# Gathering experts' tokens for two pairs at once from an fp32r copy of h, and scattering a pair's output in one block

## The chip, the cores and the metric

One core of a Trainium2 chip runs the whole kernel. The metric is the time of one execution in microseconds (us), the median of several runs. Lower is better.

## The reference

Two layers work on 512 tokens of 1024 channels in fp32. Each layer has a mixer (attention beside a convolution in the first, a short convolution in the second) and then a mixture of 16 experts in which each expert chooses its own 64 tokens. The change concerns the experts alone:

```python
def ec_moe(h, w_r, w_gate, w_up, w_down):
    bsz, n, _ = h.shape
    cap = max(1, EC_CAPACITY * n // N_EXPERTS)          # 2 * 512 // 16 = 64
    aff = jax.nn.softmax(jnp.einsum("bnd,de->bne", h, w_r).astype(jnp.float32), axis=-1)
    gates, idx = lax.top_k(jnp.swapaxes(aff, 1, 2), cap)
    bidx = jnp.broadcast_to(jnp.arange(bsz)[:, None, None], idx.shape)
    xs = h[bidx, idx]
    hid = jax.nn.silu(jnp.einsum("becd,edf->becf", xs, w_gate)) * jnp.einsum("becd,edf->becf", xs, w_up)
    ys = jnp.einsum("becf,efd->becd", hid, w_down) * gates[..., None].astype(h.dtype)
    return jnp.zeros_like(h).at[bidx, idx].add(ys)
# per layer: h = h + m5 * ec_moe(modulate(rms_norm(h), m3, m4), ...)
```

## The kernel before

Tokens lie on the partitions in four tiles of 128 (`h[t]`). In each layer `moe` first routes: VectorE finds every expert's 64 tokens and gives each chosen token a place from 1 to 64 (`slot`). Experts then go in eight pairs, expert 0 to 15 in order. `one_hot(pair)` makes a matrix of zeros and ones that picks a pair's 2 x 64 tokens; `gather` multiplies h (for the first pair h with the norm's factor in the matrix, afterwards `xr2`, a copy of h times that factor) by it on TensorE and gets the pair's tokens, channels on the partitions, in `xs`; a VectorE pass per 128 channels adds scale and shift (line 1094). An expert's gate and up products (`halves`, line 1124) read `xs` against the weights, `hid` is made, transposed (line 1166) and multiplied by the down weights. `spread` transposes the one-hot matrix into `C` and sums the pair's gates; `scatter` adds the finished pair's output back to `h`, two TensorE passes at a time between the down products of the next even expert (line 1175).

Weights come in loads of 1 MB (256 rows of a 1024 x 1024 matrix). An expert has twelve: gate 0 to 3, up 4 to 7, down 8 to 11; "load n" below counts them through a layer from 0, so expert e has loads 12e to 12e+11. All are issued by SyncE (SP) in that order, far ahead of their use: an issue waits only until the buffer that it writes is no longer read. Buffers come from three pools: `ring` (5), `w` (3) and `big` (9), and for loads 2 and 3 from `p`. `SLOT` deals them out:

```python
j = (i if i < 2 else i - 2 if i < 17 else i - 4) % 15
return BIG(shape) if i in (17, 18) or j >= 8 else RING(shape) if j < 5 else W(shape)
```

So loads 0 to 18 have buffers of their own (all 9 of `big` among them), and from load 19 on a cycle of 15 runs: 5 `ring`, 3 `w`, 7 `big`. The two others of `big` hold `xr2` from expert 1 on. From load 27 on, load n waits until TensorE has read load n - 15 (loads 19 to 26 wait for one read earlier still). The order of work on each engine is the order in which the code is written (`manual_schedule`).

Of the kernel before, what the change touches and what calls it, by code (L numbers as in the profile page):

```python
# [50 lines left out]
def backbone(ctx, tc, x, c, cx, c_ctx, ada_w, ada_b, norm1_g, norm2_g, ev_w_in, ev_q_g, ev_k_g,  # L51
# [66 lines left out]
    def EARLY(*dims):  # L118
        """What only the first mixer needs; its buffer goes to the experts' weights afterwards."""
# [367 lines left out]
    # every step of the mixer by name, with the steps that must be emitted before it  # L487
# [70 lines left out]
    # rms over heads, rope  # L558
# [412 lines left out]
    def moe(l, setup, route):  # L971
# [14 lines left out]
        afp = SM([128, NT, 32], tag="af", bufs=1)  # token tiles in the order 0, 2, 1, 3  # L986
# [11 lines left out]
        # an expert's 64th largest: each half of the tokens (its own partitions) in falling order, then  # L998
        # max(A[i], B[63 - i]) are the 64 largest of both
# [24 lines left out]
        # how many are larger, in every partition: their count on the diagonal, summed over the partitions  # L1024
# [4 lines left out]
        # the larger ones count first, then those equal to it; a count above 64 gets no place  # L1029
# [19 lines left out]
        xr2 = []  # L1049

        def one_hot(pair, scale=None):
            m_ = T([128, NT, 128])
            for t in range(NT):
                for par in range(2):
                    e = 2 * pair + par
                    o = m_[:, t, par * 64:par * 64 + 64]
                    if scale is None:
                        dve.tensor_scalar(o, iota[:, 1:65], slot[:, t, e:e + 1], None, op0=OP.is_equal)
                    else:
                        dve.tensor_scalar(o, iota[:, 1:65], slot[:, t, e:e + 1], scale(t, e), op0=OP.is_equal,  # L1060
                                          op1=OP.mult)
            return m_

        def spread(pair, m_):
            p = PB([128, NT, 128])
            for t in range(NT):
                pe.transpose(p[:, t], m_[:, t], ident)
# [315 lines left out]
```

## Time and profile before

| what | value |
|---|---|
| median of 3 runs (lowest, highest) | 1653.07 us (1652.53, 1658.62) |
| span of the profiled execution, first to last instruction | 1649.7 us |
| median time less that span | 3.4 us |
| TensorE busy | 1495.5 us, 91% of the span |
| VectorE, ScalarE, GpSimd busy | 43%, 17%, 16% |
| moved by DMA | 488.79 MB, mean 296 GB/s |

The profiled execution's own time is not listed apart; its span is 3.4 us under the median of the runs, which is taken here as what lies around the span. Busy time of TensorE is modelled from the starts of its instructions, so it says that work was queued, not that it ran at peak. The experts of the first layer take the stretch from about 424 to 910 us, those of the second that from 1148 to 1635 us.

### The profile page before, as it was taken

Reading aid. Unit: us, or ns where it says so; the run is one execution under the profiler, and the core shown is the slowest. Engines: PE = TensorE matmul, PEld = TensorE weight load, DVE = VectorE, ACT = ScalarE, POOL = GpSimd, SP = SyncE. Lnnn points to the kernel's source line nnn. Section 1 sums busy time; section 2 is a strip of 40 time slices with the busy share of each in tenths; the row PEclk is TensorE's granted clock in tenths of the full one; section 3 lists DMA queues with packets and bytes.
Section 4 is the critical chain, followed back from the end, with each engine's and each line's share of the span. In section 5 each row is a group of like instructions: output and inputs, shape, how many; then the busy total and the mean of one; then the engine's idle time right before and its main releaser. Section 6 shows DMA issues by size and latency. Waiting matters only on the chain. (4 is left out here: it accounts for less than half of the span.)

```text
span 1649.7 us, 19217 instructions
## 1 busy us (share of the span) xinstructions
PE 1495.5 (91%) x7771; PEld 811.8 (49%) x7771; DVE 716.2 (43%) x1421; ACT 287.8 (17%) x489; POOL 263.3 (16%) x199
## 2 busy tenths in 40 slices
PE   4887989888799999999998799996999999999995
PEld 2676644477443444344342577795444344434431
DVE  1999757543422323322321899525123232332223
ACT  2423223333010000010000422221110000001002
POOL 1656233531000000000000434440000000000001
PEclk9998979889799999999999999997999999999998
DMA  9643214045799999999999247538799999999993
GB/s 326 242 158 115 90 51 153 0 179 194 293 339 411 408 409 409 409 409 409 409 409 392 94 172 264 176 131 328 264 397 409 409 409 409 409 409 409 409 407 131
DMA packets 143795, 488.79 MB, mean 296 GB/s; under 512 B 7756, under 2 KB 35708, under 8 KB 137564
## 3 DMA queue, kind: packets, MB, share of 16 engines
q1 hardware_dynamic: 142976, 486.57, 76.3%
q8 instruction: 61, 1.00, 0.2%
q0 software_dynamic: 336, 0.85, 0.2%
q10 hardware_dynamic: 396, 0.16, 0.0%
q14 instruction: 26, 0.21, 0.0%
HBM read 485.45 MB, written 2.10 MB: 296 GB/s over the span
## 5 line engine op out<-in xcount | busy, mean ns | idle before, releaser
L1124 PE MATMUL pb<-big,t 128*64 128x512 f32 x912 | 200.8, 592 | 0.0
L1150 DVE TENSOR_TENSOR t<-t,pb 128x512 f32<-128x512 f32 x32 | 22.0, 688 | 332.9 <-PE pb L1124 311.0
L1124 PE MATMUL pb<-ring,t 128*64 128x512 f32 x704 | 157.8, 595 | 2.3 <-DMA ring<-in_moe_w_up_dram 2.3
L1105 DVE TENSOR_TENSOR hall<-hall,pb 128x512 f32<-128x512 f32 x128 | 87.3, 687 | 111.7 <-PE pb L1104 111.7
L350 POOL TENSOR_TENSOR w<-ring,w 128x1024 fp32r<-128x1024 f32 x44 | 111.8, 2550 | 122.1 <-ACT w L349 122.1
L1124 PEld LDWEIGHTS pb<-big,t 128*64 128x64 f32 x912 | 65.5, 137 | 130.2 <-issue 124.5
L1124 PE MATMUL pb<-big,p 128*64 128x512 f32 x464 | 113.9, 606 | 5.7 <-ACT p L1168 5.7
L350 POOL TENSOR_TENSOR w<-big,w 128x1024 fp32r<-128x1024 f32 x10 | 24.6, 2481 | 569.3 <-DMA ring<-in_ada_w_dram 525.2
L373 PE MATMUL pa<-w,big 128*128 128x256 f32 x368 | 106.8, 290 | 1.3 <-DVE big L739 0.8
L1091 PEld LDWEIGHTS pa<-t,big 128*128 128x128 f32 x896 | 101.1, 192 | 11.4 <-issue 11.4
L477 DVE SCALAR_TENSOR_TENSOR t<-t,ring,t 128x497 f32<-128x497 f32 (+14 forms) x116 | 106.5, 982 | 0.1
L375 PE MATMUL pa<-w,big 128*128 128x256 f32 x368 | 105.2, 286 | 0.6 <-DVE big L363 0.4
L374 PE MATMUL pa<-w,big 128*128 128x256 f32 x368 | 105.2, 286 | 0.0
L1091 PE MATMUL pa<-t,big 128*128 128x128 f32 x896 | 103.8, 277 | 0.0
L373 PE MATMUL pb<-big,w 128*128 128x512 f32 x248 | 99.8, 402 | 3.5 <-DVE big L362 3.2
L375 PE MATMUL pb<-big,w 128*128 128x512 f32 x248 | 98.7, 398 | 2.5 <-POOL w L350 2.5
L1124 PEld LDWEIGHTS pb<-ring,t 128*64 128x64 f32 x704 | 50.0, 138 | 102.8 <-issue 91.5
L374 PE MATMUL pb<-big,w 128*128 128x512 f32 x248 | 98.7, 398 | 1.4 <-POOL big L363 1.2
L1104 PE MATMUL pb<-p,t 128*128 128x512 f32 x256 | 92.8, 448 | 5.1 <-ACT p L1080 3.9
L1181 DVE TENSOR_TENSOR p<-pb,G 64x512 f32<-64x512 f32 x60 | 41.3, 688 | 117.1 <-PE pb L1124 100.4
L1124 PE MATMUL pb<-w,t 128*64 128x512 f32 x400 | 89.5, 593 | 0.0
L1094 DVE TENSOR_SCALAR t<-pa,a,mT 128x128 f32<-128x128 f32 x128 | 44.3, 404 | 94.7 <-PE pa L1091 94.7
(289 smaller groups left out, 2055.5 us busy)
## 6 DMA issues: line engine op xcount, KB each, us to landing
big<-in_moe_w_gate_dram SPq DMA_DIRECT2D x60, 1024.0 KB, 18.3
big<-in_moe_w_down_dram SPq DMA_DIRECT2D x58, 1024.0 KB, 18.3
big<-in_moe_w_up_dram SPq DMA_DIRECT2D x54, 1024.0 KB, 18.3
ring<-in_ada_w_dram SPq DMA_DIRECT2D x48, 1024.0 KB, 6.8
ring<-in_moe_w_up_dram SPq DMA_DIRECT2D x48, 1024.0 KB, 18.2
ring<-in_moe_w_down_dram SPq DMA_DIRECT2D x42, 1024.0 KB, 18.3
ring<-in_moe_w_gate_dram SPq DMA_DIRECT2D x40, 1024.0 KB, 18.3
w<-in_moe_w_down_dram SPq DMA_DIRECT2D x28, 1024.0 KB, 18.3
```

Of the source, the lines that this page charges most:

```text
L350: pool.tensor_tensor(lo, src, hi.bitcast(F32), op=OP.subtract)
L373: pe.matmul(o, ah, bh, start=first and i == 0, stop=False)
L374: pe.matmul(o, ah, bl, start=False, stop=False)
L375: pe.matmul(o, al, bh, start=False, stop=last and i == n - 1)
L477: dve.scalar_tensor_tensor(acc, gp[:, a + k - MID:b + k - MID], vcT[:, k * 4 + j:k * 4 + j + 1], acc, op0=OP.mult, op1=OP.add)
L1091: pe.matmul(pa[k // 4][:, k % 4], (xr2 if pair else h)[t][:, k * 128:(k + 1) * 128], Pm[:, t], start=(t == 0), stop=(t == NT - 1))
L1094: dve.tensor_scalar(xs[k // 4][:, k % 4], pa[k // 4][:, k % 4], a2[:, k:k + 1], sh2[:, k:k + 1], op0=OP.mult, op1=OP.add)
L1104: pe.matmul(p, C[:, t * 128:(t + 1) * 128], y[:, dh], start=(y is yh), stop=(y is yl))
L1105: dve.tensor_tensor(h[t][:, ds], h[t][:, ds], p, op=OP.add)
L1124: pe.matmul(ps[64 * f:64 * f + 64, :], lhs, w[:, f * 512:(f + 1) * 512], start=(k == 0), stop=(k == KD - 1), tile_position=(0, 64 * f))
L1150: dve.tensor_tensor(hid, sl.rearrange("p (a b) -> p a b", b=128), pgu[1].rearrange("p (a b) -> p a b", b=128), op=OP.mult)
L1181: dve.tensor_tensor(y[ps_, dh], po[hs], G5[hs, ds], op=OP.mult)
```

## The change

The gather works for groups of pairs: pair 0 alone, then pairs 1 and 2, 3 and 4, 5 and 6, then pair 7 alone. `terms` keeps h times the norm's factor as two fp32r terms (`xh2`, and what is left in `xl2`) in four buffers of `big` where `xr2` had two, and a gather multiplies both terms by a one-hot matrix of up to 256 columns. `SLOT` deals loads from 19 on in a cycle of 13 (5 `ring`, 3 `w`, 5 `big`). The first pair's one-hot matrix is made without the norm's factor and then multiplied by it (`gather_first`). One VectorE operation compares all of a matrix's columns of a token tile. The gates are also split in two fp32r terms (`afs`). A pair's scatter stands in one block between the next even expert's up products and its transposes (`scatter_rows`, two banks of PSUM and one add per token tile). A group's last pair has its `spread` in its odd expert. The loads' issues are written ahead of their use by `load_next`; their order on SP is as before.

```diff
@@ SLOT
         j = (i if i < 2 else i - 2 if i < 17 else i - 4) % 15
+        if i > 18:
+            j = (i - 19) % 13
         return BIG(shape) if i in (17, 18) or j >= 8 else RING(shape) if j < 5 else W(shape)
@@ moe
-        xr2 = []
+        xh2, xl2 = [], []
+        afs = SM([128, NT, 2, NE], F32R, tag="afs", bufs=1)
+        dve.tensor_copy(afs[:, :, 0], af)
+        dve.tensor_tensor(afs[:, :, 1], af, afs[:, :, 0].bitcast(F32), op=OP.subtract)
+        def one_hot(p0, n):
+            ms = [T([128, 2, n * 128], F32R) for _ in range(2)]
+            for t in range(NT):
+                o = ms[t // 2][:, t % 2].rearrange("p (e s) -> p e s", s=64)
+                dve.tensor_tensor(o, iota[:, None, 1:65].to_broadcast([128, 2 * n, 64]),
+                                  slot[:, t, 2 * p0:2 * p0 + 2 * n][:, :, None].to_broadcast([128, 2 * n, 64]),
+                                  op=OP.is_equal)
+            return ms
@@ spread
-                pe.matmul(pg, m_[:, t], af[:, 2 * (t % 2) + t // 2, 2 * pair:2 * pair + 2], start=(t == 0), stop=(t == NT - 1))
+                pe.matmul(pg, ms[t // 2][:, t % 2, c], afs[:, 2 * (t % 2) + t // 2, :, 2 * pair:2 * pair + 2],
+                          start=(t == 0), stop=(t == NT - 1))
@@ gather
+        def gather_first(ms):
+            m_ = T([128, NT, 128])
+            for t in range(NT):
+                dve.tensor_scalar(m_[:, t], ms[t // 2][:, t % 2].bitcast(F32), rstd[:, t:t + 1], None, op0=OP.mult)
...
+        def terms():
+            for x in (xh2, xl2):
+                xr = [BIG([128, 2, D], F32R) for _ in range(2)]
+                x += [xr[t // 2][:, t % 2] for t in range(NT)]
+            for t in range(NT):
+                act.activation(xh2[t], h[t], AF.Copy, scale=rstd[:, t:t + 1])
+                dve.scalar_tensor_tensor(xl2[t], h[t], rstd[:, t:t + 1], xh2[t].bitcast(F32), op0=OP.mult,
+                                         op1=OP.subtract)
+        def gather(ms, n):
+            pa = [PA([128, 4, n * 128]) for _ in range(2)]
+            xs = [C4([128, 2, 256]) for _ in range(4)]
+            for k in (0, 2, 4, 6, 1, 3, 5, 7):
+                for t in range(NT):
+                    for x in (xh2, xl2):
+                        pe.matmul(pa[k // 4][:, k % 4], x[t][:, k * 128:(k + 1) * 128], ms[t // 2][:, t % 2],
+                                  start=(t == 0 and x is xh2), stop=(t == NT - 1 and x is xl2))
+                modulated(pa, xs, k, n * 128)
+            return xs
@@ scatter
+        def scatter_rows(C, yh, yl, t):
+            p = PA([128, 2, 512])
+            for dh in range(2):
+                for y in (yh, yl):
+                    pe.matmul(p[:, dh], C[:, t * 128:(t + 1) * 128], y[:, dh], start=(y is yh), stop=(y is yl))
+            dve.tensor_tensor(h[t], h[t], p.rearrange("p a b -> p (a b)"), op=OP.add)
@@ loop over pairs and experts
+        groups = {0: 1, 1: 2, 3: 2, 5: 2, 7: 1}
+        while slots[0] < 19:
+            load_next()
+        hot, first_pair = one_hot(0, 1), 0
+        xs, part = gather_first(hot)
...
+                        if e == 1 and src is moe_w_gate and k == 4:
+                            terms()
...
-                if par == 0:
-                    C, gate = spread(pair, hot)
-                if par == 1 and pair + 1 < NE // 2:
-                    cur = gather(pair + 1, hot)
-                    cur[1](range(KD))
+                if par == 0 and prev is not None:
+                    for t in range(NT):
+                        scatter_rows(*prev, t)
+                ahead_of = par == 1 and pair + 1 in groups
+                if par == (0 if pair + 1 in groups else 1):
+                    C, gate = spread(pair, hot, pair - first_pair)
+                if ahead_of:
+                    xs = gather(following, groups[pair + 1])
+                    hot = following
...
                 for k, w in chunks(moe_w_down, e):
-                    if par == 0 and prev is not None:
-                        scatter(*prev, (k // 2,), (k % 2,))
                     halves(po, hT[:, k % 4, (k // 4) * 64:(k // 4) * 64 + 64], w, k)
```

Three places show how instructions move. The first is the SP queue of the first layer, loads 26 to 35 (gate of expert 2 from its third load, its up and its down). Before:

```order
L1117 DMA w_3395<-in_moe_w_gate_dram 128x2x1024
L1117 DMA big_3401<-in_moe_w_gate_dram 128x2x1024
L1117 DMA big_3417<-in_moe_w_up_dram 128x2x1024
L1117 DMA big_3423<-in_moe_w_up_dram 128x2x1024
L1117 DMA big_3429<-in_moe_w_up_dram 128x2x1024
L1117 DMA big_3435<-in_moe_w_up_dram 128x2x1024
L1117 DMA big_3469<-in_moe_w_down_dram 128x2x1024
L1117 DMA big_3483<-in_moe_w_down_dram 128x2x1024
L1117 DMA ring_3497<-in_moe_w_down_dram 128x2x1024
L1117 DMA ring_3511<-in_moe_w_down_dram 128x2x1024
```

The same ten loads with the change:

```order
L1162 DMA w_3430<-in_moe_w_gate_dram 128x2x1024
L1162 DMA big_3436<-in_moe_w_gate_dram 128x2x1024
L1162 DMA big_3443<-in_moe_w_up_dram 128x2x1024
L1162 DMA big_3449<-in_moe_w_up_dram 128x2x1024
L1162 DMA big_3455<-in_moe_w_up_dram 128x2x1024
L1162 DMA big_3461<-in_moe_w_up_dram 128x2x1024
L1162 DMA ring_3504<-in_moe_w_down_dram 128x2x1024
L1162 DMA ring_3510<-in_moe_w_down_dram 128x2x1024
L1162 DMA ring_3516<-in_moe_w_down_dram 128x2x1024
L1162 DMA ring_3522<-in_moe_w_down_dram 128x2x1024
```

The order of the loads stays; `big` now serves five of them where it served seven, so loads 32 and 33 take ring buffers that loads 19 and 20 filled, and load 35 waits for the reading of load 22 instead of load 20.

The second place is VectorE between the end of routing and the first gather (`slot` is written by the row of `sm_3047`, the one-hot matrices are `t_3049` before, `t_3094`, `t_3095` and `t_3100` now). Before:

```order
L1046 TENSOR_TENSOR t_3045<-pb_3039,sm_3036 128x128
L1048 TENSOR_TENSOR sm_3047<-t_3045 128x64
L1060 TENSOR_SCALAR t_3049<-iota,sm_3047,sm_2969 128x64 x8
L1094 TENSOR_SCALAR t_3060<-pa_3058,a_0_2238,mT_147 128x128 x2
L1094 TENSOR_SCALAR t_3061<-pa_3059,a_0_2238,mT_147 128x128
```

With the change:

```order
L1048 TENSOR_TENSOR t_3045<-pb_3039,sm_3036 128x128
L1050 TENSOR_TENSOR sm_3047<-t_3045 128x64
L1054 CAST sm_3049<-t_2987 128x4x16
L1055 TENSOR_TENSOR sm_3049<-t_2987,sm_3049 128x4x16
L1062 TENSOR_TENSOR t_3094<-iota,sm_3047 128x128 x2
L1062 TENSOR_TENSOR t_3095<-iota,sm_3047 128x128 x2
L1097 TENSOR_SCALAR t_3100<-t_3094,sm_2969 128x128 x2
L1097 TENSOR_SCALAR t_3100<-t_3095,sm_2969 128x128 x2
L1090 TENSOR_SCALAR t_3107<-pa_3105,a_0_2238,mT_147 128x128 x2
```

The first matrix that TensorE reads (the first of `t_3049` before, the first of `t_3100` now) stood second behind `slot`, two operations of 64 columns making it; now it stands seventh.

The third place is TensorE from the end of expert 2's up products to its down products (`C` is `t_3184` before, `t_3204` now; `p_3376`, `p_3377` and `p_3411`, `p_3412` are pair 0's output in two terms). Before:

```order
L1124 MATMUL pb_3416<-big_3435,t_3301 64x512 x4
L1067 MATMUL pb_3445<-ident,t_3403 128x128 x4
L1072 MATMUL pb_3452<-sm_2987,t_3403 128x2 x4
L1166 MATMUL pb_3460<-ident,t_3443 128x128 x4
L1104 MATMUL pb_3471<-p_3376,t_3184 128x512
L1104 MATMUL pb_3471<-p_3377,t_3184 128x512
L1124 MATMUL pb_3468<-big_3469,p_3465 64x512 x2
L1104 MATMUL pb_3477<-p_3376,t_3184 128x512
L1104 MATMUL pb_3477<-p_3377,t_3184 128x512
L1124 MATMUL pb_3468<-big_3469,p_3465 64x512 x2
```

With the change:

```order
L1176 MATMUL pb_3442<-big_3461,t_3304 64x512 x4
L1146 MATMUL pa_3471<-p_3411,t_3204 128x512
L1146 MATMUL pa_3471<-p_3412,t_3204 128x512
...
L1146 MATMUL pa_3489<-p_3411,t_3204 128x512
L1146 MATMUL pa_3489<-p_3412,t_3204 128x512
L1225 MATMUL pb_3495<-ident,t_3469 128x128 x4
L1176 MATMUL pb_3503<-ring_3504,p_3500 64x512 x4
L1176 MATMUL pb_3503<-ring_3510,p_3500 64x512 x4
```

All sixteen scatter passes now stand ahead of the transposes and the down products follow each other; this expert's spread (L1067, L1072) has gone to expert 3.

## Rows read from the trace of the kernel before

**Rows 1.** The page's head.

```profile
span 1649.7 us, 19217 instructions
```

**Rows 2.** Busy time by stretch: length, then each engine, TensorE's clock, DMA share, GB/s.

```profile
425.00:445.00 20.00, 20.00 (x108) 12.32 (x109) 4.78 (x19) 1.88 (x2) 0.00 (x0) 0.87 0.52 184
445.00:465.00 20.00, 17.77 (x88) 7.03 (x86) 4.97 (x15) 2.25 (x4) 0.00 (x0) 1.00 0.86 317
465.00:485.00 20.00, 19.32 (x124) 11.34 (x122) 3.42 (x10) 5.33 (x6) 0.00 (x0) 1.00 0.99 386
485.00:500.00 15.00, 15.00 (x72) 5.00 (x70) 4.16 (x12) 2.04 (x3) 0.00 (x0) 1.00 0.95 353
500.00:880.00 380.00, 374.08 (x1884) 158.17 (x1882) 108.98 (x265) 28.14 (x45) 0.00 (x0) 1.00 1.03 409
1160.00:1180.00 20.00, 17.77 (x94) 8.16 (x92) 4.23 (x15) 4.13 (x6) 0.00 (x0) 1.00 0.70 260
...
1215.00:1605.00 390.00, 384.08 (x1930) 161.32 (x1926) 113.12 (x277) 30.18 (x48) 0.65 (x1) 1.00 1.03 409
```

**Rows 3.** DMA issues: KB each and median us from issue to landing.

```profile
big<-in_moe_w_gate_dram SPq DMA_DIRECT2D x60, 1024.0 KB, 18.3
...
ring<-in_sc_w_out_dram SPq DMA_DIRECT2D x4, 1024.0 KB, 4.9
```

**Rows 4.** Chain that ended last, pairs 2 and 3 of layer 1: start, us, what.

```profile
1258.01 7.36 PE pa L1091 x64
...
1266.46 20.82 PE pb L1124 x96
...
1291.62 1.01 PE pb L1124 x4
1292.63 0.67 PE pb L1104 x2
...
1316.40 7.36 PE pa L1091 x64
```

**Rows 5.** TensorE in order of time: products with each layer's last up load.

```profile
884.34 1.94 PE L1124 MATMUL pb<-ring,t 128*64 128x512 f32 x8 [0.62 <-DMA ring<-in_moe_w_up_dram]
...
1608.22 1.94 PE L1124 MATMUL pb<-ring,t 128*64 128x512 f32 x8 [0.64 <-DMA ring<-in_moe_w_up_dram]
```

**Rows 6.** SP queue in order of time, both layers: issues from the first's start.

```profile
463.86 0.37 SPq L1117 DMA_DIRECT2D big<-in_moe_w_gate_dram  x1
...
475.88 10.76 SPq L1117 DMA_DIRECT2D ring<-in_moe_w_down_dram  x2
...
1199.65 10.76 SPq L1117 DMA_DIRECT2D ring<-in_moe_w_down_dram  x2
```

**Rows 7.** TensorE in order of time, experts 0 and 1 of layer 0.

```profile
424.19 5.55 PE L1091 MATMUL pa<-t,hall 128*128 128x128 f32 x24 [1.22 <-DVE t L1060]
...
452.89 0.95 PE L1072 MATMUL pb<-sm,t 128*128 128x2 f32 x8
453.70 0.63 PE L1166 MATMUL pb<-ident,t 128*128 128x128 f32 x4
...
475.76 7.41 PE L1091 MATMUL pa<-t,big 128*128 128x128 f32 x64
...
484.29 7.09 PE L1124 MATMUL pb<-ring,p 128*64 128x512 f32 x32 [0.68 <-ACT p L1168]
```

**Rows 8.** VectorE in order of time, end of layer 0's routing.

```profile
423.00 0.29 DVE L1046 TENSOR_TENSOR t<-pb,sm 128x128 f32<-128x128 f32 x1 [0.70 <-PE pb L1044]
423.33 0.23 DVE L1048 TENSOR_TENSOR sm<-t 128x64 f32<-128x64 f32 x1
423.59 1.88 DVE L1060 TENSOR_SCALAR t<-iota,sm,sm 128x64 f32<-128x64 f32 x8
```

**Rows 9.** TensorE in order of time: fp32r products of 256 columns in the mixer.

```profile
400.69 0.28 PE L373 MATMUL pa<-w,big 128*128 128x256 f32 x1
400.81 0.28 PE L374 MATMUL pa<-w,big 128*128 128x256 f32 x1
```

More of the change, by code (lines that the diff above doesn't have):

```diff
@@ L1082, in split_out, with modulated @@
                                          op1=OP.subtract)
-        def gather(pair, Pm):
+        def modulated(pa, xs, k, n):
+            dve.tensor_scalar(xs[k // 2][:, k % 2, 0:n], pa[k // 4][:, k % 4], a2[:, k:k + 1], sh2[:, k:k + 1],
+                              op0=OP.mult, op1=OP.add)
+        def gather_first(ms):
+            m_ = T([128, NT, 128])
+            for t in range(NT):
+                dve.tensor_scalar(m_[:, t], ms[t // 2][:, t % 2].bitcast(F32), rstd[:, t:t + 1], None, op0=OP.mult)
             pa = [PA([128, 4, 128]) for _ in range(2)]
-            xs = [C4([128, 4, 128]) for _ in range(2)]
+            xs = [C4([128, 2, 256]) for _ in range(4)]
             def part(ks):
@@ L1106, in scatter, with load_next @@
                     next(beside, None)
+        def scatter_rows(C, yh, yl, t):
[4 more added lines that the diff above has]
+            dve.tensor_tensor(h[t], h[t], p.rearrange("p a b -> p (a b)"), op=OP.add)
+        loads = [(src, e, kk) for e in range(NE) for src in (moe_w_gate, moe_w_up, moe_w_down)
+                 for kk in range(0, KD, 2) if e < NE - 1 or src is not moe_w_down]
+        ahead = {}
+        def load_next():
+            src, e, kk = loads.pop(0)
+            if slots[0] in (2, 3):
+                slots[0] += 1
+                ws = [P3([128, D]) for _ in range(2)]
+                for k in range(2):
+                    nc.sync.dma_start(ws[k], src[l, e, (kk + k) * 128:(kk + k + 1) * 128, :])
+            else:
+                w = SLOT([128, 2, D])
+                nc.sync.dma_start(w, src[l, e, kk * 128:(kk + 2) * 128, :].rearrange("(k p) n -> p k n", p=128))
+                ws = [w[:, k] for k in range(2)]
+            ahead[id(src), e, kk] = ws
         def chunks(src, e):
             for kk in range(0, KD, 2):
-                if slots[0] in (2, 3):
-                    slots[0] += 1
-                    ws = [P3([128, D]) for _ in range(2)]
-                    for k in range(2):
-                        nc.sync.dma_start(ws[k], src[l, e, (kk + k) * 128:(kk + k + 1) * 128, :])
-                else:
-                    w = SLOT([128, 2, D])
-                    nc.sync.dma_start(w, src[l, e, kk * 128:(kk + 2) * 128, :].rearrange("(k p) n -> p k n", p=128))
-                    ws = [w[:, k] for k in range(2)]
+                while (id(src), e, kk) not in ahead:
+                    load_next()
+                ws = ahead.pop((id(src), e, kk))
                 for k in range(2):
@@ L1131, in moe @@
         for pair in range(NE // 2):
-            xs, part = cur
+            if pair in groups:
+                first_pair = pair
             for par in range(2):
@@ L1139, in moe @@
                     for k, w in chunks(src, e):
-                        if k == 6 and src is moe_w_gate and (par == 0 or pair + 1 < NE // 2):
-                            hot = one_hot(pair + par)
+                        if k == 6 and src is moe_w_gate and par and pair + 1 in groups:
+                            following = one_hot(pair + 1, groups[pair + 1])
                         if e == 0 and src is moe_w_gate:
```

37 lines of the change are left out of this document (12 added, 25 removed).

## Prediction

> **What bounds the kernel now.** I read the page's head for the span [rows 1], then the busy time by stretch through both layers' experts [rows 2]. From 500 to 880 us and again from 1215 to 1605 us two things are full at once: TensorE is busy 374 of 380 and 384 of 390 us, and the DMA engines move 409 GB/s at a share of 1.03. Only one of the two can hold the other back over such a stretch, so the question is which.
>
> The landing times answer it [rows 3]: a 1 MB load of gate weights lands 18.3 us after its issue, while the same size lands in 4.9 us where the queue is short. At 409 GB/s a load of 1.0486 MB takes 2.56 us, so some seven loads stand in the queue when one is issued. The DMA engines therefore have work waiting throughout and 409 GB/s is what they give. Twenty-four loads, a pair of experts, take 61.5 us.
>
> TensorE's own pace is in the chain [rows 4]: from one gather's start to the next 1316.40 - 1258.01 = 58.4 us a pair. It is 3.1 us a pair faster than the weights arrive, and lives on what was loaded ahead. That stock runs out just at the end: with the last up load of either layer TensorE waits for the DMA, by 0.62 and 0.64 us [rows 5]. From there to the end of the run lies a tail that begins when that load lands. So each layer's experts end when DMA is through, and **what moves the end is the point from which the DMA engines are never idle again**, plus 2.56 us for every load not yet done there.
>
> That point is in the SP queue [rows 6]. Two issues of ring loads start at 475.88 us and take 10.76 us together: load 34 goes at once, load 35 only at 475.88 + 10.76 - 0.37 = 486.27 us (0.37 us is what a single issue takes, as at 463.86 us). It waits for load 20 to be read, the first of expert 1's down products, which begin at 484.29 us and read a load every 7.09 / 4 = 1.77 us [rows 7]. In layer 1 the same issue comes at 1199.65 + 10.39 = 1210.04 us. Load 27 was issued at 463.86 us, and loads 27 to 34 are 20.5 us of DMA work, so the engines ran dry at about 484.4 us, 1.9 us before load 35. Up to 500 us the rows show 184 to 386 and 353 GB/s, afterwards 409 [rows 2].
>
> **The change, part by part.**
>
> *Two weight buffers fewer.* `terms` takes four of `big` instead of two, at expert 1. Loads 27 to 31 now wait for loads 14 to 18 to be read, not 12 to 16, and load 33 for load 20. The DMA stop at the gather of expert 1 thus comes with load 33 instead of load 35: loads 27 to 32 are six, 15.4 us of work, and begin two reads of 20.82 / 12 = 1.74 us [rows 4] and the start's delay (below) after 463.86 us, so the engines run dry at about 484 us as before. When load 20 has been read, two loads more are still to do: 2 x 2.56 = 5.1 us later for load 35 and all behind it. Nothing hides this, because DMA has no idle time after it. Bounds: 0 if holes remained after 500 us that could take the two loads up; 5.1 otherwise. The rows at 409 throughout say 5.1.
>
> *VectorE before the first gather.* TensorE waits 1.22 us for the one-hot matrix [rows 7], of which it needs the first token tile: 2 of the 8 operations that take 1.88 us, 0.47 us [rows 8]. Now come two small ones for `afs` (0.23 each by L1048), four comparisons of 128 columns (0.29 each by L1046) and one scaling (0.27, between the two): 0.46 + 1.16 + 0.27 = 1.89 us, 1.4 us more. TensorE, SP's waits on its reads, and every load from 19 on come 1.4 us later, since the buffers were full and DMA idle at 425 us [rows 2]. No such comparison with two spread operands is in the trace; priced as 64-column ones (0.235) it is 1.2 more, priced at 0.4 it would be 2.0 more. I take 1.4.
>
> *Gates.* Four fp32r passes instead of eight fp32 ones of 0.81 / 8 = 0.10 us (452.89 to 453.70 us, [rows 7]): 0.4 us less in expert 0; at the lower bound nothing.
>
> *Gather of expert 1.* Before, 64 passes of 128 columns take 7.36 us [rows 4] (7.41 with the last one's end, [rows 7]). Now 64 passes of 256 columns, fp32r, serve two pairs. The mixer's passes of that form start every 0.12 us [rows 9]: 7.7 us, 0.3 more. At the price of the old pass it is 0; were they twice as long it would be 8.0 more, but the form is the same. The terms themselves (four ScalarE copies, four VectorE operations) lie beside the gate and up products between load 13 and the gather, six loads of 1.74 us: each of the four would have to take over 2 us to be late, and then the gather waits for what is over.
>
> *Later pairs.* Three gathers of 7.7 us replace six of 7.36 (3.5 us a pair saved). The scatter took 8 x 0.67 us between down products [rows 4], 5.4 us; in a block it is at most that plus a wait for VectorE's adds. So a pair takes TensorE about 55 us or less instead of 58.4. This does not reach the end: TensorE gains 6 us and more a pair on the weights, uses its stock up several pairs earlier, and from there waits for each load. Its next wait is DMA, in steps of about a microsecond.
>
> *Tail.* The last pair's spread now stands between the last up products and the transposes. Four transposes (0.63 us for such four, [rows 7]) and four small passes of 0.1 lie beside the making of `hid`, for which TensorE waits anyway; I add 0.1 us, with 0 and the whole 1.0 as bounds.
>
> Sum for a layer: 5.1 + 1.4 - 0.4 + 0.3 + 0.1 = 6.5 us; both layers have the same order and the same stop, so 13 us. Span 1649.7 + 13.0 = 1662.7 us, and with 3.4 us around it, as between this span and the median, **1666 us**.
>
> **Rivals.**
>
> *DMA follows TensorE (faster).* If 409 GB/s were TensorE's pace and the DMA engines had room, saved TensorE time would count: six pairs by 3.5, seven scatters by about 1, eight gates by 0.4, 31 us a layer, less the 1.4 of the start: 1653 - 2 x 30 = 1593 us. It decides as soon as loads land in clearly under 18.3 us while TensorE doesn't wait. Against it: the queue of seven loads, and the waits for DMA at both layers' ends [rows 3, 5]. The Trainium skill ("DMA: Bandwidth & Descriptors", section Bandwidth, Measured) gives 425 GB/s for a large transfer with the pair's other core idle; were that to be had here, the 157 loads from 35 to the end would take 387 instead of 402 us in each layer and the time would be about 1636 us, an estimate from that page's figure. The trace doesn't agree that more than 409 is left, since these 409 are moved with work waiting.
>
> *The missing buffers cost nothing (about the same).* If DMA could make up the two loads, only the start's 1.4 us and the tail stay: 1653 + 3 = 1656 us. For it speaks that the buffers bind only in a layer's first two pairs. Against it: a stop of DMA there isn't made up behind a queue that never empties [rows 2, 3].
>
> *TensorE's clock falls while it waits (slower still).* It is granted 0.87 at 425 to 445 us, after routing has left TensorE idle, and 1.00 wherever it is busy [rows 2]. With 6 us or more of waits in each 61.5 us it would be less busy than now; at 1.2 GHz a load's two products take 3.5 instead of 1.74 us [rows 4], more than the 2.56 of DMA. If that held for the last expert's eight gate and up loads, it adds 8 x 0.9 = 7 us a layer: 1680 us. Against it: 1.00 from 1160 to 1180 us with only 17.77 of 20 us busy.
>
> **How the numbers follow.** The forecast's case has 0.75, DMA following TensorE 0.06, no cost of the buffers 0.11, the clock 0.08. The forecast's own range is its bounds: per layer 5.1 + 1.2 - 0.4 at least and 5.1 + 2.0 + 0.3 + 1.0 at most, 11.8 to 16.8 us, 1665 to 1670; the small terms' neighbours and runs 0.3% apart make it 1660 to 1671. To leave out no more than 2 in 10 the range runs from 1655 to 1678. A change of 0.5%, 8.3 us, is about what a measurement can tell from none: above 1661.3 lie the forecast (most of it) and the clock, 0.80; within, the rest of the forecast and the costless buffers, 0.13; below 1644.8 the first rival and a little more, 0.07.
>
> **What would show it.** In the profile after: the ring issue for load 33 ends its wait when expert 1's first down load has been read, and the next stretch at 409 GB/s has begun 1 to 2 us later than before; load 35 is issued about 4 to 5 us after 486.27 us; loads land after 18 us from then on, and TensorE's waits for DMA are no longer only at the layers' ends [rows 5] but tens of microseconds, spread over each layer's second half; the last up load lands 6 to 7 us later in layer 0 and 13 in layer 1. The first gather starts 1.4 us later than 424.19 us. The prediction is wrong if the stretches run above 412 GB/s, if the DMA engines pause in them, or if TensorE's clock in the last pair is under 1.00.

## The result and the profile after

The changed kernel takes 1678.86 us (median of 4 runs, 1676.49 to 1683.2) against 1654.84 us for the kernel before on the same chip (1652.53 to 1658.62): ratio 1.014, 95% interval 1.011 to 1.0169. It is slower, as forecast, but by 24 us instead of 13; the forecast of 1666 us is missed and the top of its range, 1678, too.

The page's head for the kernel after, to be held against [rows 1]:

```profile
span 1678.2 us, 17923 instructions
PE 1457.1 (87%) x7323; PEld 786.6 (47%) x7323; DVE 679.8 (41%) x1121; ACT 288.1 (17%) x489; POOL 263.0 (16%) x199
```

TensorE has 38 us less to do than before (1457.1 against 1495.5 us) and the profiled span is 28.5 us longer. The stretches after (columns as in [rows 2]: busy time of each engine, granted clock as a part of 2.4 GHz, DMA share, GB/s):

```profile
485.00:500.00 15.00, 13.05 (x74) 6.68 (x75) 3.79 (x8) 1.48 (x3) 0.00 (x0) 1.00 0.57 195
500.00:520.00 20.00, 18.88 (x88) 7.78 (x86) 6.73 (x7) 1.73 (x3) 0.00 (x0) 1.00 1.02 412
520.00:880.00 360.00, 324.11 (x1530) 132.31 (x1528) 79.22 (x120) 26.39 (x42) 0.00 (x0) 0.98 1.03 409
842.00:850.00 8.00, 6.57 (x29) 5.93 (x28) 1.64 (x4) 0.39 (x1) 0.00 (x0) 0.52 1.03 410
850.00:858.00 8.00, 7.75 (x24) 2.40 (x26) 0.00 (x0) 0.20 (x1) 0.00 (x0) 0.63 1.02 408
1240.00:1620.00 380.00, 342.12 (x1610) 140.48 (x1608) 84.61 (x125) 27.13 (x44) 0.65 (x1) 0.98 1.03 409
```

TensorE is now busy 90% of the long stretches instead of 98 to 100%, and DMA still moves 409 GB/s: it is DMA that sets the pace. Two things are new. The stretch that is not full reaches on to 500 us, at 195 GB/s. And from 842 to 858 us TensorE's clock is granted at 0.52 and 0.63, near its lower level of 1.2 GHz; in layer 1 the same comes at 1576 us.

The SP queue at DMA's stop, layer 0 and layer 1, answers to [rows 6]:

```profile
478.76 18.27 SPq L1162 DMA_DIRECT2D ring<-in_moe_w_down_dram  x4
1212.99 18.29 SPq L1162 DMA_DIRECT2D ring<-in_moe_w_down_dram  x4
```

The first of each four is load 32, the others are 33 to 35. Load 36 goes at 498.4 us, and each of the last three 1.72 us behind the one ahead, so load 33 goes at 493.2 us. As predicted it is load 33 that has to wait now, not 35 ("the stop" below is this wait of DMA's queue). But it goes 6.9 us later than load 35 did (486.27 us), not one or two. The reason stands in TensorE's timeline at the end of expert 1 (start, duration, line, operation, count, and in brackets the idle time ahead with what ended it):

```profile
478.65 1.21 PE L1127 MATMUL pa<-t,big 128*128 128x256 f32 x8
480.49 2.17 PE L1127 MATMUL pa<-t,big 128*128 128x256 f32 x16 [0.64 <-DVE t L1090]
483.30 2.17 PE L1127 MATMUL pa<-t,big 128*128 128x256 f32 x16 [0.64 <-DVE t L1090]
486.11 2.17 PE L1127 MATMUL pa<-t,big 128*128 128x256 f32 x16 [0.64 <-DVE t L1090]
488.92 1.22 PE L1127 MATMUL pa<-t,big 128*128 128x256 f32 x8 [0.64 <-DVE t L1090]
489.98 0.60 PE L1225 MATMUL pb<-ident,t 128*128 128x128 f32 x4
491.25 7.09 PE L1176 MATMUL pb<-ring,p 128*64 128x512 f32 x32 [0.68 <-ACT p L1227]
```

The gather of expert 1 takes 478.65 to 489.98, 11.3 us, where [rows 7] have 7.4. Four times TensorE waits 0.64 us for VectorE's pass over a channel block (line 1090); these waits are called holes below. The middle of a layer looks as predicted; the end doesn't. TensorE in the middle, and from pair 7's gather on:

```profile
798.26 1.94 PE L1176 MATMUL pb<-ring,t 128*64 128x512 f32 x8 [0.62 <-DMA ring<-in_moe_w_up_dram]
800.82 1.94 PE L1176 MATMUL pb<-ring,t 128*64 128x512 f32 x8 [0.62 <-DMA ring<-in_moe_w_up_dram]
...
835.93 1.11 PE L1127 MATMUL pa<-t,big 128*128 128x128 f32 x8
837.54 2.00 PE L1127 MATMUL pa<-t,big 128*128 128x128 f32 x16 [0.51 <-DVE t L1090]
840.05 2.00 PE L1127 MATMUL pa<-t,big 128*128 128x128 f32 x16 [0.51 <-DVE t L1090]
842.56 3.67 PE L1127 MATMUL pa<-t,big 128*128 128x128 f32 x16 [0.50 <-DVE t L1090]
846.73 1.97 PE L1127 MATMUL pa<-t,big 128*128 128x128 f32 x8 [0.50 <-DVE t L1090]
848.50 1.08 PE L1225 MATMUL pb<-ident,t 128*128 128x128 f32 x4
850.25 8.16 PE L1176 MATMUL pb<-ring,p 128*64 128x512 f32 x24 [0.67 <-ACT p L1227]
...
886.71 5.32 PE L1176 MATMUL pb<-w,t 128*64 128x512 f32 x24
891.86 8.75 PE L1176 MATMUL pb<-big,t 128*64 128x512 f32 x40
```

In the middle each load's eight passes wait 0.62 us for it, 2.56 us apart: that is DMA's pace. Pair 7's gather takes 12.6 us with four such holes, its passes go from 0.125 to 0.23 us apart (3.67 us for 16) as the clock falls, and the transposes and down products behind it are slow too. Afterwards TensorE no longer waits for a single load up to the layer's end: forty passes stand back to back where [rows 5] have a wait for the last load. TensorE lags behind DMA there.

Where the time went is best seen between four marks in each layer: the copy of the router's logits (line 975 before, 977 after), the first pass of the first gather, the issue at DMA's stop (load 35 before, 33 after), and the start of expert 15's `hid`. All are starts of instructions in the traces, layer 0 / layer 1, in us; a run has one trace, so a difference of some tenths between runs says little:

| kernel | logits to first gather | to the stop's load | to expert 15's hid | sum |
|---|---|---|---|---|
| before | 16.3 / 16.3 | 62.1 / 61.9 | 400.1 / 400.2 | 478.5 / 478.4 |
| after | 18.4 / 18.2 | 64.8 / 64.5 | 407.5 / 408.4 | 490.7 / 491.1 |
| predicted difference | 1.4 | -0.1 | 5.1 | 6.4 |
| measured difference | 2.1 / 1.9 | 2.7 / 2.6 | 7.4 / 8.2 | 12.2 / 12.7 |
| e1, blocks alternate | 18.8 / 18.8 | 61.8 / 61.1 | 404.5 / 406.7 | 485.1 / 486.6 |
| e2, before with 13 | 16.3 / 16.6 | 60.5 / 62.0 | 404.8 / 407.0 | 481.6 / 485.6 |
| e3, late groups | 18.5 / 18.1 | 66.3 / 69.0 | 405.2 / 407.6 | 490.0 / 494.7 |
| e4, table early | 17.2 / 16.8 | 65.4 / 64.7 | 408.8 / 407.4 | 491.4 / 488.9 |
| e13, both of e1 and e3 | 18.1 / 18.5 | 60.3 / 60.9 | 403.9 / 406.9 | 482.3 / 486.3 |
| e9, before with products in routing | 16.3 / 16.4 | 59.8 / 59.8 | 400.2 / 401.2 | 476.3 / 477.4 |

The two layers' differences make 24.9 us, the median's is 24.0. (The span's 28.5 has 2.1 us of the first mixer and 3.0 us of the run's end besides, less 1.3 between the layers, which vary from run to run as much.)

### The profile page after: what moved, and what is told of

The parts are those of the page before. It is cut to its first block, busy times and chain, and to the rows that moved or that the text cites. A ratio compares the mean times of both kernels' runs of the same rounds, so it can differ in the third digit from the quotient of the medians.

```text
span 1678.2 us, 17923 instructions
## 1 busy us (share of the span) xinstructions
PE 1457.1 (87%) x7323; PEld 786.6 (47%) x7323; DVE 679.8 (41%) x1121; ACT 288.1 (17%) x489; POOL 263.0 (16%) x199
## 5 line engine op out<-in xcount | busy, mean ns | idle before, releaser
L1176 PE MATMUL pb<-big,t 128*64 128x512 f32 x832 | 186.6, 594 | 11.0 <-DMA big<-in_moe_w_gate_dram 7.1
L1176 PE MATMUL pb<-ring,t 128*64 128x512 f32 x736 | 169.4, 597 | 18.3 <-DMA ring<-in_moe_w_up_dram 14.2
L1176 PEld LDWEIGHTS pb<-big,t 128*64 128x64 f32 x832 | 58.5, 137 | 135.0 <-issue 106.8
L1176 PE MATMUL pb<-w,t 128*64 128x512 f32 x448 | 101.7, 594 | 5.3 <-DMA w<-in_moe_w_up_dram 5.3
L1176 PE MATMUL pb<-ring,p 128*64 128x512 f32 x384 | 90.4, 620 | 8.3 <-ACT p L1227 8.3
L1127 PE MATMUL pa<-t,big 128*128 128x256 f32 (+1 forms) x512 | 76.2, 303 | 19.3 <-DVE t L1090 19.3
L1176 PE MATMUL pb<-big,p 128*64 128x512 f32 x352 | 79.8, 596 | 8.1 <-ACT p L1227 6.9
L1127 PEld LDWEIGHTS pa<-t,big 128*128 128x128 f32 x512 | 68.5, 206 | 32.0 <-DVE t L1090 25.5
L375 PEld LDWEIGHTS pa<-w,big 128*128 128x128 f32 x368 | 72.4, 197 | 3.0 <-DVE big L741 1.0
## 6 DMA issues: line engine op xcount, KB each, us to landing
big<-in_moe_w_gate_dram SPq DMA_DIRECT2D x50, 1024.0 KB, 18.7
ring<-in_moe_w_up_dram SPq DMA_DIRECT2D x48, 1024.0 KB, 18.5
```

What stands on the lines that cost most here:

```text
L375: pe.matmul(o, ah, bh, start=first and i == 0, stop=False)
L1127: pe.matmul(pa[k // 4][:, k % 4], x[t][:, k * 128:(k + 1) * 128], ms[t // 2][:, t % 2], start=(t == 0 and x is xh2), stop=(t == NT - 1 and ...
L1176: pe.matmul(ps[64 * f:64 * f + 64, :], lhs, w[:, f * 512:(f + 1) * 512], start=(k == 0), stop=(k == KD - 1), tile_position=(0, 64 * f))
```

## The experiments

The theory after the result: from the stop on a layer runs at DMA's pace, as predicted; the surplus of some 12 us is the holes in the gathers (at expert 1 directly, at pair 7 because TensorE then lags to the layer's end) and a slower start. Rivals: the fp32r gather is dear in itself; the surplus comes from the scatter in a block; the buffers cost another amount than 5.1 us. The ratios below are each against the kernel before on the same chip; the changed kernel's own is 1.014 [1.011, 1.0169].

**e1: no block behind another of its tile.**

```diff
-            for k in (0, 2, 4, 6, 1, 3, 5, 7):
+            for k in (0, 4, 2, 6, 1, 5, 3, 7):
```

> The changed kernel with one edit: the gather's channel blocks go in the order 0, 4, 2, 6, 1, 5, 3, 7, so that no block follows another of the same PSUM tile. Theory: the waits of 0.64 us for VectorE in expert 1's gather (four of them) are waits for a whole PSUM tile and vanish; the gather takes 8.7 us instead of 11.3, load 33 is issued 2.6 us earlier in each layer, and since the DMA engines then have no idle time, the end comes 2.6 us earlier per layer. The same four waits in pair 7's gather (2.0 us) stand where TensorE lags at the layer's end, so up to 2.0 more per layer. Together 5 to 9 us less than the changed kernel: 1670 to 1674 us, ratio to the kernel before 1.009 to 1.0115. Rival (the waits only cover another limit, such as VectorE's own pace or DMA): no change from the changed kernel, ratio 1.014.

1670.78 us, ratio 1.0118 [1.0088, 1.0149], just above the expected band. The interval overlaps the changed kernel's, so the two ratios alone don't tell them apart; by the marks it is 5.6 and 4.5 us a layer less, and e4 below, which keeps the holes and was measured beside it, ran from 1673.79 us up where e1 ran from 1668.16 to 1673.9. TensorE in this run, expert 1's gather, pair 7's, and the last weights of layer 0:

```profile
480.54 7.94 PE L1127 MATMUL pa<-t,big 128*128 128x256 f32 x64
488.32 0.60 PE L1225 MATMUL pb<-ident,t 128*128 128x128 f32 x4
...
834.74 7.09 PE L1127 MATMUL pa<-t,big 128*128 128x128 f32 x62
...
891.43 1.94 PE L1176 MATMUL pb<-big,t 128*64 128x512 f32 x8 [0.63 <-DMA big<-in_moe_w_up_dram]
894.02 1.94 PE L1176 MATMUL pb<-big,t 128*64 128x512 f32 x8 [0.66 <-DMA big<-in_moe_w_up_dram]
```

No wait is left in either gather, and the waits for DMA are back at the end. The gather of two pairs takes 7.8 us to the transposes' start: the 7.7 that the prediction gave it. The holes were a wait for a whole tile: `pa` is two tiles of four channel blocks, with 256 columns blocks 0 and 2 lie in different banks of the first, and block 2 waited for VectorE to have read block 0. The Trainium skill ("PSUM — Partial Sum Buffer", section PSUM bank collisions raise a hardware error) asks for a guard by bank and quadrant of partitions; by that block 2 need not have waited for block 0, and the trace shows that at 256 columns it did. With 128 columns a tile's four blocks are 512 numbers a partition, one bank (`scatter_rows` has two of that size), so there that guard would ask for the wait too.

**e2: two buffers fewer, and nothing else.** In the kernel before:

```diff
+        if i > 18:
+            j = (i - 19) % 13
...
-                    xr = [BIG([128, 2, D]) for _ in range(2)]
-                    xr2 += [xr[t // 2][:, t % 2] for t in range(NT)]
+                    xr = [BIG([128, 2, D]) for _ in range(4)]
+                    xr2 += [xr[t][:, 0] for t in range(NT)]
```

> The kernel before with one part of the change: two buffers of big fewer for the weights. The copy of h lies in four buffers of big (a token tile in each, the other half of each unused) and loads from 19 on go in the cycle of 13. Gather, scatter and routing are those of before. Theory: load 33 instead of 35 waits for expert 1's first down load, two loads of 2.56 us more are left behind it, and nothing makes them up: 5.1 us per layer, 10.3 in all, ratio to the kernel before 1.006, load 33 issued within 0.5 us of 486.27 us. Rival (the buffers cost nothing because DMA makes the loads up later): ratio 1.000, under 2 us.

1665.77 us, ratio 1.0084 [1.0054, 1.0113]. In SP's queue load 33 now has to wait, until 486.96 us; it is the second of the four, and the others follow 1.72 us apart:

```profile
476.57 14.19 SPq L1119 DMA_DIRECT2D ring<-in_moe_w_down_dram  x4
492.11 0.37 SPq L1119 DMA_DIRECT2D ring<-in_moe_w_gate_dram  x1
```

From load 33 to expert 15's `hid` it is 4.7 and 6.8 us more than from load 35 before; 5.1 was said. The interval of the time (8.9 to 18.7 us) includes the 10.3 of the two layers; its middle lies above them. Layer 1 of this trace holds something else besides the buffers:

```profile
1588.68 2.57 PE L1126 MATMUL pb<-ring,t 128*64 128x512 f32 x8 [1.97 <-DMA ring<-in_moe_w_up_dram]
1589.80:1596.60 6.80, 6.80 (x26) 4.00 (x22) 1.69 (x4) 1.17 (x2) 0.00 (x0) 0.50 1.02 408
```

One load came late, TensorE waited 1.97 us for it, and its clock was 0.50 for the next 6.8 us. In expert 15 TensorE then waits for no load, and `hid` starts 3.5 us after the last up load has landed, where before it was 2.1 us. If these 1.4 us are what TensorE lost there, 5.4 us are left for layer 1, and the buffers' term holds.

**e3: the single pairs are 0 and 1.**

```diff
-        groups = {0: 1, 1: 2, 3: 2, 5: 2, 7: 1}
+        groups = {0: 1, 1: 1, 2: 2, 4: 2, 6: 2}
```

> The changed kernel with one line altered: the groups are pair 0, pair 1, then pairs 2 and 3, 4 and 5, 6 and 7, instead of the single pairs being 0 and 7. The gather at expert 1 is thus of 128 columns and the last gather stands in expert 11, not 13. Theory: at expert 1 the gather takes some 7 us with its waits instead of 11.3, so load 33 comes 3 to 5 us earlier; and the last pair's TensorE lag at the layer's end (2.7 us behind the last load) goes. 5.5 to 7.5 us per layer, 11 to 15 in all: 1664 to 1668 us, ratio 1.0055 to 1.008. Rival (the lag at the end is from the scatter block and the spread, not from the gather before it): only the 3 to 5 us at expert 1, 6 to 10 in all, ratio 1.008 to 1.0105, and TensorE still without DMA waits in expert 15. Second rival (the time follows TensorE's work): no change, since the passes are as many.

1683.07 us, ratio 1.019 [1.0155, 1.0225]: a clear miss, and if anything in the wrong direction. The layer's end gained 2.3 and 0.8 us (405.2 and 407.6 in the table), and TensorE waits for DMA in expert 15 again. But the gather of half the columns, now at expert 1, took 10.9 and 13.9 us and load 33 went later. TensorE in layer 1:

```profile
1206.74 1.11 PE L1127 MATMUL pa<-t,big 128*128 128x128 f32 x8
1208.36 2.00 PE L1127 MATMUL pa<-t,big 128*128 128x128 f32 x16 [0.51 <-DVE t L1090]
1210.86 3.27 PE L1127 MATMUL pa<-t,big 128*128 128x128 f32 x16 [0.50 <-DVE t L1090]
1214.64 3.68 PE L1127 MATMUL pa<-t,big 128*128 128x128 f32 x16 [0.50 <-DVE t L1090]
1218.82 1.97 PE L1127 MATMUL pa<-t,big 128*128 128x128 f32 x8 [0.51 <-DVE t L1090]
```

and its stretches there:

```profile
1211.00:1219.00 8.00, 6.99 (x33) 6.62 (x34) 1.64 (x4) 0.00 (x0) 0.00 (x0) 0.52 0.63 253
1219.00:1225.00 6.00, 5.32 (x20) 3.08 (x22) 0.41 (x1) 0.59 (x1) 0.00 (x0) 0.50 0.01 3
```

It is the picture of pair 7's gather in the changed kernel: holes of 0.5 us, then 0.52 of the clock; here, at the stop, DMA runs idle besides. The gathers of 256 columns had holes of 0.64 us and kept their 1.00. The traces of the changed kernel, e3 and e4, which keep the holes, agree: the clock fell to 0.50 in all six gathers of 128 columns with holes and in none of the eighteen of 256. The Trainium skill ("TensorE: Matmul & The Clock Gate", section A second HAM failure mode: psum-queue depth-cycling) tells of a bf16 kernel whose short idles between groups of matmuls made the clock go back and forth; this trace agrees as far as short idles came before a fall, to 0.52, but the clock fell once in a gather and did not go back and forth.

**e13: e1 and e3 together.** The edits are those two.

> The changed kernel with both the groups 0, 1, 2 and 3, 4 and 5, 6 and 7 (run e3) and the blocks' order 0, 4, 2, 6, 1, 5, 3, 7 (run e1). Theory: run e3 did not gain because expert 1's gather of 128 columns has four or five holes of 0.5 us, in which TensorE's clock falls to 1.2 GHz; without the waits it stays at 2.4 GHz and the gather takes 7.1 us. So this run is 0 to 2 us faster than run e1, where the same gather takes 7.9: ratio 1.0105 to 1.012, and the granted clock is 1.00 at both gathers. Rival (128 columns at expert 1 are slow in themselves): as run e3, 1.019, and a clock under 0.9 at expert 1's gather.

1666.95 us, ratio 1.0076 [1.0045, 1.0107], faster than the expected band of 1.0105 to 1.012. Without the holes the same gather of 128 columns takes 7.2 us, and the clock is 1.00 from 477 to 485 us:

```profile
477.61 7.36 PE L1127 MATMUL pa<-t,big 128*128 128x128 f32 x64
484.81 0.63 PE L1225 MATMUL pb<-ident,t 128*128 128x128 f32 x4
```

e3 and e13 differ in the blocks' order alone, and their intervals lie apart: e3 failed by its holes, not by its columns. This kernel, the change without holes and with its last gather two experts earlier, is 12.6 us slower than before by the ratio. That this is nearly the 13 us of the prediction is in part luck, since the parts differ: about 2.0 us a layer at the start, 1.5 less up to the stop and 5.2 more behind it, where 1.4, 0.1 less and 5.1 were predicted.

**e4: the table of Exp ahead of time.**

```diff
         act.copy(lg, pl)
+        act.activation(SM([128, 1]), ident[:, 0:1], AF.Exp)
```

> The changed kernel with one instruction added: a ScalarE Exp of one constant column right after the logits are copied, so that the table for Exp is loaded while VectorE makes the softmax's argument. Theory: the table load of 1.28 us, which in the changed kernel waits for VectorE, goes off the way to the first gather; the first gather begins 1.1 to 1.3 us earlier in each layer, and the end 2.4 us in all: ratio lower by 0.0014 than that of the changed kernel. Rival (another wait has the same end): the first gather begins no earlier.

In the trace the first gather comes 1.3 and 1.4 us sooner after the logits, as expected. The time, 1681.75 us, ratio 1.0181 [1.0147, 1.0214], shows no gain; the runs of this kernel, which keeps the holes, spread from 1673.79 (the profiled one) to 1687.44 us, and an effect of 2.4 us is not to be seen in them. What ScalarE does in the changed kernel:

```profile
409.98 0.27 ACT L977 COPY t<-pb 128x128 f32<-128x128 f32 x1 [0.87 <-PE pb L955]
412.43 1.28 ACT L994 ACT_TABLE_LOAD   x1 [2.18 <-DVE t L991]
413.73 0.26 ACT L994 ACTIVATE t<-t 128x64 f32<-128x64 f32 x1
```

Before, the table load stood right behind the copy and only the Exp waited for VectorE:

```profile
407.88 0.27 ACT L975 COPY t<-pb 128x128 f32<-128x128 f32 x1 [0.87 <-PE pb L953]
408.16 1.28 ACT L992 ACT_TABLE_LOAD   x1
410.28 0.26 ACT L992 ACTIVATE sm<-sm 128x64 f32<-128x64 f32 x1 [0.84 <-DVE sm L989]
```

The change moved `afp` from a buffer of its own to a pooled one (`T`). Now the table load itself waits for VectorE: 1.28 us more on the way to the first gather. That the pool is the cause was not tried apart and is not shown; e4 shows the price alone.

**e8: the scatter in one block, alone.** The kernel before with `scatter_rows` in place of `scatter`, ahead of the next even expert's `spread`.

> The kernel before with one part of the change: a pair's scatter in one block ahead of the next even expert's spread and transposes, with two banks and one add for each token tile. Theory: TensorE's time in the middle of a layer isn't on the path, so nothing changes: ratio 0.999 to 1.001. Rival (the block's waits for VectorE's add, 0.4 us, and its place right before the transposes delay the layer's end): 1 us or more for each layer, ratio 1.0015 or more. Second rival (TensorE's work counts): seven blocks save about 1 us each, ratio 0.992.

1653.7 us, ratio 1.0013 [0.9983, 1.0043]. No change that can be measured, and in its trace the sum to expert 15's `hid` is 476.4 and 478.2 us, 2.1 and 0.2 less than before. The second rival, 0.992, is excluded; the first, 1.0015 or more, is not by the time alone, but the sums speak against it.

**e5: most of the gather among the down products.** The changed kernel with e1's order and

```diff
+                    for i in range(2):
+                        block(BLOCKS[i])
...
                 for k, w in chunks(moe_w_down, e):
+                    if ahead_of and k >= 2:
+                        block(BLOCKS[k])
```

> The changed kernel with the gather's blocks in the order 0, 4, 2, 6, 1, 5, 3, 7, and only two of them ahead of the odd expert's transposes; the six others stand among its down products, ahead of those of k = 2 to 7. Theory: DMA's last stop in a layer is set by the latest of (issue of load n less 2.56 n); with the gather in one block that is load 33, with it among the downs load 33 comes some 6 us earlier and load 36 at the same time as before, and load 36 then decides: 2.6 us less per layer than with the order alone (run e1), 5 us in all, ratio to the kernel before 1.0075 to 1.0095. Rival (the time follows how long TensorE works up to expert 2, not the place of the stop): as with the order alone, 1.0118.

1667.64 us, ratio 1.0082 [1.0051, 1.0113], in the expected band. Load 33 goes at 484.9 us and load 36 at 497.8; the sum to expert 15's `hid` is 483.0 and 485.4 us, 2.1 and 1.2 less than e1's where 2.6 was expected; the intervals of e1 and e5 overlap, so the time alone doesn't show the gain. While TensorE keeps up, what counts is the load for which the issue's time less 2.56 us for every load ahead of it is latest: load 36 here, 33 in e1.

**e10: the kernel before with the gather among the down products and products in routing.**

```diff
+        pw = PB([128, 512])
+        for _ in range(13):
+            pe.matmul(pw, ident, h[0][:, 0:512], start=True, stop=True)
...
+        for _ in range(2):
+            pe.matmul(pw, ident, h[0][:, 0:512], start=True, stop=True)
         place = T([128, NT, 2, NE])
...
-                    cur[1](range(KD))
+                    for i in range(2):
+                        cur[1](BLOCKS[i:i + 1])
...
+                    if par == 1 and k >= 2:
+                        cur[1](BLOCKS[k:k + 1])
```

> The kernel before with two edits that follow from the theory: the gather's blocks in the order 0, 4, 1, 5, 2, 6, 3, 7, two ahead of the odd expert's transposes and six among its down products, and 15 products of the identity with h[0] during routing whose result nobody reads, for TensorE's clock. Theory: the stop at load 35 costs 1.9 us a layer and goes; the first gather at 2.4 instead of 1.2 GHz reads the first load 2.5 to 3 us earlier, and all loads come as much earlier. 4.4 to 4.9 us a layer, 9 to 10 in all, ratio 0.994 to 0.9945. Rival (the end of a layer is set by TensorE): ratio 1.000 or above.

1681.39 us, ratio 1.0158 [1.0121, 1.0196]: a clear miss, on the side of the rival named there. TensorE's timeline, routing and the end of layer 0:

```profile
409.27 13.80 PE L1005 MATMUL pb<-hall,ident 128*128 128x512 f32 x26
423.00 0.47 PE L1025 MATMUL pb<-ident,t 64*128 64x64 f32 x4
...
884.50 7.04 PE L1129 MATMUL pb<-big,t 128*64 128x512 f32 x32
891.36 7.04 PE L1129 MATMUL pb<-ring,t 128*64 128x512 f32 x32
```

The products ran 13.8 us, longer than the 9.1 us for which TensorE waits for VectorE's search before, so the first gather came 4.6 and 5.0 us later after the logits (20.9 and 21.3 against 16.3). And in the last expert TensorE waits for no load: from load 35 to `hid` it is 418.4 us instead of 400.1. Some 5 us of that are a later stop, at load 38; `hid` starts 14.3 and 12.4 us later than before after the last landings (loads 185 and 187). From expert 1's gather to the end of its down products it needs 17.5 us (475.02 to 492.54) where it needed 15.4 in one block (476.06 to 491.50, run e9), some 0.3 us for each of seven blocks. Seven such gathers make 14.7 us a layer, and the kernel before, where TensorE is just ahead of DMA at the layer's end, had no such time to spare. What each of the two edits costs was not tried apart in this kernel.

**e6: all edits on the changed kernel,** with e10's fifteen products.

> The changed kernel with everything that the runs so far point to: the gather among the down products with its blocks alternating, groups of pairs 0, 1, then 2 and 3, 4 and 5, 6 and 7, the Exp table loaded early, afs made after the first gather's matrix, and 15 products of the identity with h[0] during routing whose result nobody reads, so that TensorE's clock is at 2.4 GHz when the first gather begins. Theory: against run e5 the first load is read 1.3 us (table) + 0.4 us (afs) + 2.5 to 3 us (clock) earlier, and the gather of expert 1 has cheaper passes (0.11 us for 128 columns against 0.124), 0.8 us: 5 to 5.5 us per layer, 10 to 11 in all; ratio to the kernel before 1.001 to 1.004. The two missing buffers of 5.1 us a layer remain. Rival (the clock doesn't rise for such products, or the start doesn't count): 1.006 or more.

1667.75 us, ratio 1.0077 [1.0051, 1.0103]: missed. The products take 13.9 us in layer 0, and from the logits to the first gather it is 21.0 and 20.0 us.

**e12: the same with nine products,** eight in VectorE's search and one ahead of the gather, and only expert 1's gather among the down products.

> The changed kernel as in run e6, with nine products for the clock instead of fifteen, and only expert 1's gather among the down products (the later ones in one block, with their channel blocks alternating). Theory: against run e6 the routing's transposes come some 4 us earlier in each layer, and so do all loads from 19 on; ratio to the kernel before 1.001 to 1.004. What is left over the kernel before is the 5.1 us a layer of the two buffers, less what the start gains. Rival (the routing's delay was not on the path in run e6): 1.0077 as there.

1659.9 us, ratio 1.0039 [1.0009, 1.007], in the band. The best version of the change that was tried is still behind the kernel before.

**e9: the kernel before with the nine products.**

> The kernel before with nine products of the identity with h[0] during routing whose result nobody reads, eight while VectorE looks for the experts' tokens and one ahead of the first gather. Fifteen of them, in the run with both edits, took 13.8 us and made the routing's transposes some 4 us late; eight are 7.6 to 9 us, which fit in the 9.1 us for which TensorE waits there. Theory: the first gather's first part takes 2.9 us at 2.4 GHz instead of 5.55 and the first weights 1.94 instead of 2.27; load 0 is read 2.9 us earlier, load 19 and all behind it follow, and the end comes 2.9 us earlier per layer: ratio 0.996 to 0.997. Rival (the end does not follow the start, since TensorE or the mixer sets it): 1.000.

1649.61 us, ratio 0.9978 [0.9949, 1.0006]; not to be told from no change by the time, and a smaller gain than expected. The stretch at the first gather:

```profile
425.00:431.00 6.00, 5.76 (x35) 3.92 (x37) 3.56 (x14) 0.00 (x0) 0.00 (x0) 1.00 1.02 409
```

The clock is 1.00 there, the first gather's first part takes 3.54 us to the weights' start instead of 5.5, and load 35 comes 2.3 and 2.1 us sooner after the first gather. The products' results are read by nobody.

## Why the prediction was half right

**What bounds the kernel: right.** 409 GB/s in every version, with TensorE busy 90 to 100%. *DMA follows TensorE* is out: TensorE's work fell by 38 us. The 425 GB/s that the prediction cited from the Trainium skill ("DMA: Bandwidth & Descriptors", section Bandwidth, Measured) were not seen: in full stretches of 20 us and more the rows have 412 at most, as the prediction argued.

**Two weight buffers fewer: right,** in place and size. Load 33 is the one that waits, and e2 alone shows 4.7 and 6.8 us for the 5.1, or 4.7 and 5.4 without TensorE's lag in its layer 1.

**Gather of expert 1: the step that failed first.** The sum gave it 0.3 us more; measured it is 3.9 (11.3 against 7.4). The passes were priced rightly: 7.8 us in e1. Left out was that a block's pass over PSUM by VectorE is waited for by the next block of the same tile, though the order 0, 2, 4, 6 put blocks of one tile side by side, and each block is read right after its passes. The table has 2.65 us to the stop's load, since the gates (0.4, as predicted) and a first gather at a partly better clock (4.94 and 1.94 us for the 5.55 and 2.27 of before, 0.9 less) are to be taken off the 3.9.

**Later pairs: the second, at a layer's end.** The prediction put the savings there at nothing, since TensorE would use its stock up and from there wait for each load to the last. Up to pair 6 that is right: TensorE waits for DMA 37 us in all (24 times for `ring` up loads, 14.2 us), the savings don't reach the end, and e8 shows no gain from the scatter's block that can be measured. At pair 7 it fails: the gather with its holes and its fallen clock takes 12.6 us, and TensorE, which gains only 0.83 us on each load, is late to the end. `hid` starts 2.8 us later after the landing of load 185 in layer 0 and 1.7 us later after that of load 187 in layer 1 than before. Where e1 takes the holes away, 3.0 and 1.7 us come back between the stop's load and `hid`. That is the rival *the clock falls while it waits*, in a place that it did not name. It was given 0.08 and priced for the last expert's loads; there the clock is 1.00. What fell was the clock in a gather with holes just ahead of the last pair. Waits of 0.62 us for weights left it at 1.00, but behind the wait of 1.97 us in e2 it fell to 0.50.

**Tail: right.** It was put at 0.1 us; from the last `hid` to the transposes it is 0.74 us in both kernels, so the spread between them costs nothing.

**VectorE before the first gather: half.** The operations themselves cost 0.8 us, from `slot` to the first pass 1.65 instead of 0.85, not 1.4 (four comparisons take 0.89, a quarter less than priced; at 0.4 us each the prediction's own sum gives 1.9 more, not its 2.0). The other 1.3 us is the table load, which no step had looked at. That the two together, 2.0 us, lie near the 1.4 is luck.

Sum for a layer, measured: 5.1 for the buffers, 2.65 to the stop, 2.0 at the start, 2.7 at the end (7.8 less 5.1): 12.45, twice 24.9. That most of the surplus is the holes, directly and through the lag, is shown by e1's marks and by the time of e13 against e3; that the clock's fall is due to the holes is shown by e3 against e13. What stays open is why holes of 0.64 us at 256 columns leave the clock alone and holes of 0.5 at 128 don't.

## What to carry to other kernels

Where an engine writes a multi-bank PSUM tile block by block and another reads each block at once, give neighbouring blocks to different tiles; look in the order of the code for the same tile twice in a row, since such a wait is not in the trace of a kernel that reads only at the end. Work saved on an engine that is not the bound was worth nothing that could be measured here. A delay of that engine late in the stage still costs what it cannot catch up: from the start of pair 7's gather to the last eight passes of the down products behind it the changed kernel took 8.6 us longer than e1 in layer 0, and some 3 us of it reached the layer's end. And where a change touches the buffer of one instruction, look at what stands ahead of it in its queue: here a table load began to wait.

## What the hardware showed that was not expected

Behind holes of 0.50 us in a gather of 128 columns TensorE's clock was halved (0.52 from 842 to 850 us, 0.50 from 1219 to 1225 us in e3), in all six such gathers. Holes of 0.64 us in eighteen gathers of 256 columns, and 0.62 us of waiting for every load of 2.56 us, left it at 1.00. Behind a single late load it was halved too: 0.50 behind a wait of 1.97 us in e2 (1589.8 to 1596.6 us) and behind one of 2.02 us in e4 (661.9 to 665.3 us). An fp32 gather cut into blocks of 8 passes between weight products cost 2.1 us more than in one piece (e10 against e9).
